# One program, two issue orders: instructions moved within the orders of all five engines of a hybrid decoder layer

## The chip, the cores and the metric

The kernel runs on one core of a Trainium2 chip. The metric is the device time of one execution in microseconds; the time of a kernel is the median of its runs. A profiled execution also leaves a trace, whose times are us from the start of its span. TensorE (PE) does the matrix products, with its weight loads (PEld) recorded beside them; VectorE (DVE), ScalarE (ACT) and GpSimd (POOL) work on tiles; SyncE (SP) issues the transfers (DMA).

## The reference

One layer of a decoder trunk, for 1024 tokens of 1024 channels, all float32. One input projection feeds three groups of heads, whose gated outputs go through one output projection, a residual and a LayerNorm:

```python
proj = jnp.einsum("bsd,de->bse", x, w_in[l])
q, k, v, g_a, x_b, g_b, c_cols, g_c = jnp.split(proj, split_idx, axis=-1)
y_a = _swa_sinks(q, k, v, attn_sinks[l])        # sliding-window attention: 8 q heads, 2 kv heads, d=64, window 128
y_b = _rg_lru(x_b, conv_w[l], ...)              # causal conv of 4, gates, linear recurrence h = a*h + u; 256 wide
y_c, v_own = _rwkv7(c_cols, rwkv_mu[l], ...)    # RWKV-7: token shift, decay, delta-rule matrix state; 4 heads of 64
y = jnp.concatenate([y_a * silu(g_a), y_b * silu(g_b), y_c * silu(g_c)], axis=-1)
out = jnp.einsum("bse,ed->bsd", y, w_out[l])
x = _layer_norm(ALPHA * x + out, ln_g[l], ln_b[l])
```

## The kernel before

**Arithmetic.** Each large product is computed in three parts: an operand is rounded to a shorter type (`xh`, `wcah`, `w_q`, on ScalarE or VectorE), the residue is taken on VectorE (`xl`, `wcal`, the lower half of `w_q`), and TensorE adds high by high, high by low and low by high into one PSUM tile (`mm3`, line 301). A product of one weight tile has 128 rows of contraction and 512 columns, half of the tokens.

**Stages.** The tokens are done in two halves (0 and 1) of 512. First come the projections of the RWKV group of half 0, straight from the weights in `in_w_c`, in eight steps k over the channels (tile `c`, lines 345 to 372). Then, for each half, a stream of dense projections runs (`pj_q`, `pj_ga`, `pj_xb` and so on), and between its products stand those of the attention (`sp`, `tp`, `pv`), the recurrence of group B (a scan on VectorE) and the RWKV group. The RWKV group computes in chunks of 64 tokens: scores within a chunk (`sc`, from `AR` and `BK`), an inverse of a triangular matrix (`rwkv_inverse`, `rwkv_merge`, which end in the tile `Tt`), and a chain over the eight chunks (`rwkv_chain`) that carries the state `S`: `S` times a tile goes through `UV` (copied by ScalarE or VectorE), a product `ch`, its copy `u`, another product `ch`, and so on to the next state. The projected weights that both halves need are split once and kept in DRAM (`kept_q`, `kept_ga`). Last comes the output projection `o` of both halves with residual and LayerNorm on VectorE.

**Start.** The input transfers are issued by SyncE in an order of its own. TensorE begins with four products of the tile `blocks` with itself, 256 columns, whose result nobody reads (`WARM = 4`, line 341); they are TensorE's numbers 0 to 3. `con` holds the constants, the identity for the transposes among them; `par` the per-channel parameters, from which VectorE computes columns `dv` and `sc`.

**Order.** What sets the order of the work is written out by hand twice. `MERGED` (line 58) gives the order in which the generators of the stages are asked for their next piece, and with it the order in which instructions are created, the tiles and the buffers. Then, for each of the five engines, `ISSUED` (line 67) says in which order its instructions are issued. `Listed` (line 223) stands before each engine and records its instructions as they are created; the numbers in `ISSUED` are positions in that record, and "4-6" stands for 4, 5, 6. At the end of the program the lists are turned into dependencies that cost no wait:

```python
for a, b in zip(seq, seq[1:]):
    tc.add_manual_dep(b, a.name, NOSYNC, reason="order of the engine")
```

Each engine works strictly down its list; where the next instruction isn't ready, all that stand behind it wait. Since every instruction goes through the one call in `Listed`, nearly all rows of the profile name line 231: what an instruction is, its tiles say.

Of the kernel before, what the change touches and what calls it, by code (L numbers as in the profile page):

```python
# [172 lines left out]
),  # L173
"gpsimd": (
    "0 2 1 3-4 14-15 5-13 17 16 27-28 18-24 26 25 29-37 41-48 39 38 40 49-52"
),
"sync": (
# [1159 lines left out]
```

## Time and profile before

| | |
|---|---|
| median of 3 runs | 482.28 us (481.49, 482.28, 482.39) |
| profiled execution, own time | 482.19 us |
| its span in the trace | 480.4 us |
| TensorE busy | 466.0 us, 97% of the span |
| VectorE busy | 364.7 us, 76% |
| ScalarE busy | 242.4 us, 50% |
| GpSimd busy | 36.4 us, 8% |
| DMA | 71.45 MB, mean 149 GB/s |

The profiled execution is one of many; its own time is that of the device, its span the part that the trace covers. Busy time of an engine is the time in which at least one of its instructions ran. Rows of the trace give the start of an instruction in us from the span's start and how long it was busy; TensorE's products overlap, so that the distance of two starts, not the busy time, tells how fast it goes.

### The profile page before, as it was taken

Reading aid. Unit: us, or ns where it says so; the run is one execution under the profiler, and the core shown is the slowest. Engines: PE = TensorE matmul, PEld = TensorE weight load, DVE = VectorE, ACT = ScalarE, POOL = GpSimd, SP = SyncE. Lnnn points to the kernel's source line nnn. Section 1 sums busy time; section 2 is a strip of 40 time slices with the busy share of each in tenths; the row PEclk is TensorE's granted clock in tenths of the full one; section 3 lists DMA queues with packets and bytes.
Section 4 is the critical chain, followed back from the end, with each engine's and each line's share of the span. In section 5 each row is a group of like instructions: output and inputs, shape, how many; then the busy total and the mean of one; then the engine's idle time right before and its main releaser. Section 6 shows DMA issues by size and latency. Waiting matters only on the chain.

```text
span 480.4 us, 8435 instructions
## 1 busy us (share of the span) xinstructions
PE 466.0 (97%) x3088; PEld 360.8 (75%) x3088; DVE 364.7 (76%) x880; ACT 242.4 (50%) x544; POOL 36.4 (8%) x57
## 2 busy tenths in 40 slices
PE   8999999999999999999999998999999999999993
PEld 6777777777777776678778786787678778888893
DVE  5946798999998689737979669994868548636886
ACT  3427589434566798537694255329666546021000
POOL 0100000000000000000000000000002500054101
PEclk9999999999999999999999999999999999999997
DMA  8950537657766524233343484459420080120652
GB/s 275 386 200 0 196 136 264 199 130 262 268 238 130 189 91 132 89 114 128 99 167 88 141 233 153 132 119 220 134 67 24 16 283 32 64 69 0 219 176 87
DMA packets 50585, 71.45 MB, mean 149 GB/s; under 512 B 26344, under 2 KB 27624, under 8 KB 50544
## 3 DMA queue, kind: packets, MB, share of 16 engines
q1 hardware_dynamic: 50544, 70.91, 46.3%
q8 instruction: 24, 0.39, 0.4%
q14 instruction: 17, 0.14, 0.1%
HBM read 48.34 MB, written 22.56 MB: 148 GB/s over the span
## 4 chain that ended last, share of the span: by engine, by line
PE 74%; DVE 9%; ACT 7%; DMA 6%; issue 2%; SPq 1%; POOLq 0%; DVEq 0%; ACTq 0%
PE o L231 19%; PE pj_q L231 8%; PE pj_ga L231 6%; PE c L231 6%; PE pj_xb L231 3%; PE pj_gb L231 3%; PE pj_gc L231 3%; PE sp L231 3%; PE pv L231 3%; PE pj_v L231 2%; PE pj_r L231 2%; PE ch L231 2%; PE pj_av L231 2%; PE tp L231 2%; PE pj_k L231 2%
## 5 line engine op out<-in xcount | busy, mean ns | idle before, releaser
L231 PE MATMUL pj_ga<-xh,w_ga 128*128 128x512 f32 x128 | 44.0, 404 | 0.9 <-DMA w_ga<-kept_ga 0.9
L231 PE MATMUL pj_q<-xh,w_q 128*128 128x512 f32 x128 | 44.1, 403 | 0.5 <-DMA w_q<-kept_q 0.2
L231 ACT ACTIVATE s<-sp,mn 128x129 f32<-128x129 f32 x64 | 23.0, 366 | 22.0 <-DVE mn L231 21.7
L231 PE MATMUL o<-woh,yl 128*128 128x512 f32 (+1 forms) x90 | 32.5, 370 | 0.0
L231 PE MATMUL o<-woh,yh 128*128 128x512 f32 (+1 forms) x90 | 32.5, 375 | 0.0
L231 PE MATMUL o<-wol,yh 128*128 128x512 f32 (+1 forms) x90 | 32.3, 368 | 0.0
L231 PE MATMUL o<-wo,yh 128*128 128x512 f32 (+1 forms) x108 | 32.0, 374 | 0.0
L231 PEld LDWEIGHTS pj_ga<-xh,w_ga 128*128 128x128 f32 x128 | 23.6, 188 | 7.6 <-DVE it L231 1.2
L231 POOL TENSOR_TENSOR yl<-y,yh 128x512 fp32r<-128x512 f32 x16 | 20.3, 1291 | 118.0 <-PE pj_gc L231 105.5
L231 PEld LDWEIGHTS pj_q<-xh,w_q 128*128 128x128 f32 x128 | 23.8, 188 | 7.0 <-DMA w_q<-kept_q 0.7
L231 DVE SCALAR_TENSOR_TENSOR xres<-xres,o 128x512 f32<-128x512 f32 (+1 forms) x18 | 11.1, 624 | 20.3 <-PE o L231 16.2
L231 PE MATMUL pj_ga<-xl,w_ga 128*128 128x512 f32 x64 | 25.9, 405 | 0.0
L231 PE MATMUL pj_q<-xl,w_q 128*128 128x512 f32 x64 | 25.7, 401 | 0.0
L231 ACT ACTIVATE s<-s,mn 128x128 f32<-128x128 f32 x64 | 22.3, 398 | 4.3 <-DVE mn L231 4.1
L231 DVE SCALAR_TENSOR_TENSOR xres<-xres,mv,ln 128x512 f32<-128x512 f32 x32 | 22.6, 741 | 1.0 <-POOL mv L231 0.9
L231 PE MATMUL pj_gc<-xh,w_gc 128*128 128x512 f32 x64 | 23.1, 414 | 0.2 <-DVE q L231 0.2
L231 ACT CAST yh<-y 128x512 fp32r<-128x512 f32 x16 | 9.7, 618 | 26.6 <-PE o L231 22.1
L231 PEld LDWEIGHTS o<-wo,yh 128*128 128x128 f32 x108 | 19.4, 188 | 4.2 <-DVE wo L231 0.3
L231 PE MATMUL pj_gb<-xh,w_gb 128*128 128x512 f32 x64 | 21.8, 404 | 0.0
L231 PE MATMUL pj_xb<-xh,w_xb 128*128 128x512 f32 x64 | 21.8, 399 | 0.0
L231 DVE TENSOR_TENSOR PT<-tp,con 128x512 f32<-128x512 f32 x28 | 19.1, 684 | 3.4 <-PE tp L231 3.2
L231 PE MATMUL o<-wo,yl 128*128 128x512 f32 (+1 forms) x54 | 19.8, 369 | 0.0
(310 smaller groups left out, 1247.1 us busy)
## 6 DMA issues: line engine op xcount, KB each, us to landing
xr<-in_xT SPq DMA_DIRECT2D x16, 256.0 KB, 4.5
kept_ga<-w_ga SPq DMA_DIRECT2D x8, 512.0 KB, 3.2
kept_q<-w_q SPq DMA_DIRECT2D x8, 512.0 KB, 3.5
wor<-in_w_o SPq DMA_DIRECT2D x16, 256.0 KB, 2.8
w_q<-kept_q SPq DMA_DIRECT2D x8, 512.0 KB, 3.9
w_ga<-kept_ga SPq DMA_DIRECT2D x8, 512.0 KB, 4.4
xres<-in_x SPq DMA_DIRECT2D x8, 512.0 KB, 3.6
out<-xres SPq DMA_DIRECT2D x16, 256.0 KB, 2.2
```

The lines of the kernel that those rows point to most:

```text
L231: self.ins.append(getattr(self.engine, op)(*args, **kw).ins)
```

## The change

Only the five lists in `ISSUED` are replaced. The same instructions are created in the same order (2460 on TensorE, 880 on VectorE, 468 on ScalarE, 53 on GpSimd, 226 on SyncE), with the same tiles, buffers and data dependencies; only the order in which each engine takes them is another. Counted against the longest common order of the old and the new list, 499 instructions of TensorE stand elsewhere (in 410 runs of one or more), 293 of VectorE (283 runs), 150 of ScalarE (150), 7 of GpSimd (6) and 65 of SyncE (63). Most moves are short: TensorE's number 7 goes from place 4 (counted from 0) to place 0, the warm-up products 0 to 3 from places 0 to 3 to places 3, 4, 8 and 10; VectorE's 57 from place 32 to 4, its 298 from 216 to 209, its 684 from 687 to 686; ScalarE's 177 from 180 to 176, so that it stands ahead of 115; SyncE's 11 (the transfer of `con`) from 2 to 32. The diff, cut to the lines in which these stand:

```diff
@@ -66,121 +66,138 @@
...
 ISSUED = {
 "tensor": (
-    "0-3 7 10-11 8 4-6 19-20 22-23 13 24-25 21 26 39-43 9 14-15 33-35 27 44-45 53-54 28-29 47 12 30-32 50-51 48 "
...
-    "1033 1013-1016 908-911 1017-1020 1036-1039 1034-1035 1044-1046 1053-1056 1049-1052 1084-1102 1047-1048 "
...
-    "1593-1623 1836-1839 1641 1835 1840-1841 1846 1642-1644 1628-1631 1847-1850 1662-1669 1851-1854 1546 "
...
+    "7 4 13 0-1 10-11 8 2 9 3 22-23 14 5-6 15 27 19-20 24-25 21 26 33-34 39 28 35 42 40 44 16 29 47 53 41 12 "
...
+    "1011-1012 1023 1041-1042 1024 903 990-997 1025 1043 1028 1044-1046 1029-1030 1047 1033 1013-1016 908-911 "
...
+    "1823-1824 1833-1834 1624-1625 1648-1651 1626-1627 1593-1623 1836-1841 1835 1846-1847 1641-1644 1628-1631 "
...
 ),
 "vector": (
-    "55-56 78 80 77 54 79 0-1 3 2 5 4 6-8 44 10 43 9 49 53 45 42 46 51 11 52 48 47 50 12 57 103 58 73 16 59 17 "
...
-    "125 132 128 131 129 252 126 156 209 264 141 143 234 142 235 144 257 146 236 147 251 149 148 439 210 157 211 "
-    "150 212 237 290 238 372 158 239-240 159 164 160 165-168 161-163 151 441 467 152 298 153 303 154 306 155 170 "
...
-    "392 360 339-340 337 370 341 343-344 338 413 345 342 347-349 346 351 417 361 418 350 390-391 295-296 362 "
...
-    "631 637 636 660 685 661 677 683 686 721-722 688 662-663 684 664 676 665-666 691-693 689 697-698 694 699 747 "
...
+    "0 56 1-2 57 3 78 52 43 77 5 79 58 46 6 45 4 8 7 10 51 103 53 42 49 9 55 54 11-12 50 59-60 16-17 61 13 62 80 "
...
+    "109 120 122 121 110 118 203 224 123 229 135 133 145 136 134 126-127 130 124 132 137 125 138 488 222 241 207 "
...
+    "157 150 237 290 238-239 211 572 439 212 158 372 240 159 441 164 160-161 467 165 298 166 162 303 167-168 163 "
...
+    "390-391 350 418 361 295-296 362 299-300 363 301-302 417 424 382 393 326 394-395 327 329-330 396 331 425 401 "
...
+    "683 661 721-722 688 662 684 663 665 664 691 676 692-693 689 697 694 698-699 747 700-703 717-719 678 704 720 "
...
 ),
 "scalar": (
-    "1 0 2-4 26 5 17 6-7 27 55-56 8-16 18-19 21 24-25 22 31 23 30 32 28 20 29 34-35 57 59-60 58 33 62 36 38-40 42 "
...
-    "107 112 175-176 115 185 116 118 177 179 178 194-195 181 140 196-197 141 221 145 222 219 180 206 225 165 164 "
-    "226 168 182 228 171 198-199 170 202 227 183 201 203 200 205 204 229 231 188 233 232 187 207 189 208 217 "
-    "209-210 237 213 234 212 235 214 247 252 248-249 224 223 230 218 254 236 238-240 253 241 264 243-244 266 242 "
...
+    "1 0 2-4 26 5-6 17 7 27 8 55 9 56 10-16 18-19 21 31 24-25 22 32 23 20 57 30 28 34-35 59 29 33 60 58 62 36 "
...
+    "175-177 115 185 179 118 116 221 178 180 194 141 195 140 197 196 222 145 181 219 206 164-165 225-226 168 182 "
+    "228 171 198-199 202-203 170 227 201 183 207 200 229 205 204 231 208 188 187 233 232 189 217 209-210 234 212 "
+    "235 214 213 247 237 252 248-249 224 223 230 218 254 238 236 239-240 253 241 243-244 264 266 242 245 250-251 "
...
 ),
 "gpsimd": (
-    "0 2 1 3-4 14-15 5-13 17 16 27-28 18-24 26 25 29-37 41-48 39 38 40 49-52"
+    "0 2 1 3-11 13 12 16-17 14-15 18-20 28 21-27 29-37 41-48 39 38 40 49-52"
 ),
 "sync": (
-    "0 2 11 1 3-6 10 28 7-9 13 12 14-16 29-31 17-22 33 32 23-26 44-45 34 46 48 27 47 50 52 51 53-54 49 35-36 "
...
+    "0 2 1 28 10 3-7 29 8-9 13 12 14-16 30 17-20 31-32 21-23 33 24-25 44 11 26-27 45 47 34 46 48 51 35 50 49 36 "
...
 ),
 }
```

## Rows read from the trace of the kernel before

**Rows 1.** The page's first part (busy us of an engine, its share of the span, its instructions) and the first line of its fourth (the chain of work that ended last, in shares of the span).

```profile
PE 466.0 (97%) x3088; PEld 360.8 (75%) x3088; DVE 364.7 (76%) x880; ACT 242.4 (50%) x544; POOL 36.4 (8%) x57
...
PE 74%; DVE 9%; ACT 7%; DMA 6%; issue 2%; SPq 1%; POOLq 0%; DVEq 0%; ACTq 0%
```

**Rows 2.** Busy time by stage (the windows view). Columns: the stretch in us from the span's start, its length, busy us (and instructions) of TensorE, its weight loads, VectorE, ScalarE, GpSimd, the granted TensorE clock, the DMA engines' share, GB/s.

```profile
17.00:45.00 28.00, 27.82 (x119) 21.97 (x120) 18.36 (x59) 11.46 (x21) 0.00 (x0) 1.00 0.48 184
45.00:160.00 115.00, 114.22 (x674) 87.09 (x673) 104.84 (x264) 72.38 (x164) 2.84 (x11) 1.00 0.63 199
160.00:206.00 46.00, 44.57 (x521) 31.24 (x522) 35.62 (x91) 34.66 (x87) 1.04 (x2) 1.00 0.34 109
...
290.00:345.00 55.00, 52.73 (x444) 40.27 (x442) 46.11 (x129) 28.52 (x72) 0.00 (x0) 1.00 0.58 155
...
403.00:472.70 69.70, 69.69 (x348) 58.42 (x346) 48.21 (x88) 7.59 (x13) 16.32 (x15) 1.00 0.27 92
```

**Rows 3.** TensorE's first instructions (the timeline of TensorE, 0 to 9.3 us): start, busy us, output tile from input tiles, shape, instructions that the row joins, and in brackets the idle time before and what ended it.

```profile
1.48 3.78 PE L231 MATMUL c<-blocks 128*128 128x256 f32 x8 [1.48 <-POOL blocks L231]
5.00 1.22 PE L231 MATMUL c<-xh,wcah 128*128 128x512 f32 x2
...
6.87 0.63 PE L231 MATMUL c<-xh,wcah 128*128 128x512 f32 x1
7.30 0.44 PE L231 MATMUL c<-xl,wcah 128*128 128x512 f32 x1
7.58 0.39 PE L231 MATMUL c<-xh,wcal 128*128 128x512 f32 x1
7.81 0.40 PE L231 MATMUL c<-xh,wcbh 128*128 128x512 f32 x1
```

**Rows 4.** The granted clock where TensorE starts and behind its last work (the windows view; the sixth column of figures after the length is the clock, as in rows 2).

```profile
5.00:7.39 2.40, 2.40 (x7) 1.93 (x7) 1.39 (x4) 0.76 (x2) 0.00 (x0) 1.00 0.92 272
...
475.00:480.40 5.40, 0.00 (x0) 0.00 (x0) 1.83 (x3) 0.00 (x0) 0.82 (x1) 0.50 0.26 97
```

**Rows 5.** Waits and transfers of the start: TensorE's weight load near 9.20 and its products at 16.33 and 17.18 (the timeline of 0 to 20 us); VectorE's first reading of `par` (the timeline of VectorE); the transfer of `con` in the chain that ended last (start, length); TensorE's transposes of v (the timeline of TensorE).

```profile
9.20 0.19 PEld L231 LDWEIGHTS c<-xh,wcah 128*128 128x128 f32 x1 [0.50 <-ACT wcah L231]
...
16.33 0.40 PE L231 MATMUL c<-xh,wcbh 128*128 128x512 f32 x1
...
17.18 0.50 PE L231 MATMUL c<-xh,wcal 128*128 128x512 f32 x1 [0.45 <-DVE wcal L231]
...
9.79 0.16 DVE L231 TENSOR_SCALAR dv<-par 128x2 f32<-128x2 f32 x1
...
1.65 4.01 DMA con<-in_con
...
58.09 0.60 PE L231 MATMUL vtp<-con,vt 128*128 128x128 f32 x4
```

**Rows 6.** Four waits of TensorE and the instruction that each waits for (timelines around 87, 108, 202 and 340 us, columns as in rows 3; in each the product before, the product that waited, and the releaser on VectorE or ScalarE).

```profile
86.49 0.74 DVE L231 SCALAR_TENSOR_TENSOR AR<-xs_k,par,W 128x512 f32<-128x512 f32 x1
...
86.73 0.39 PE L231 MATMUL pj_q<-xh,w_q 128*128 128x512 f32 x1
...
87.38 0.83 PE L231 MATMUL sc<-AR,BK 64*128 64x128 f32 x10 [0.26 <-DVE AR L231]
...
107.35 0.69 DVE L231 TENSOR_TENSOR w_q<-wr_q,w_q 128x512 fp32r<-128x512 f32 x1
107.50 0.40 PE L231 MATMUL pj_q<-xh,w_q 128*128 128x512 f32 x1
...
108.09 0.73 PE L231 MATMUL pj_q<-xh,w_q 128*128 128x512 f32 x2 [0.20 <-DVE w_q L231]
...
202.02 0.62 PE L231 MATMUL pj_k<-xh,w_k 128*128 128x512 f32 x2
202.87 0.34 PE L231 MATMUL ch<-UV,X 128*64 128x64 f32 x4 [0.23 <-ACT UV L231]
...
202.51 0.30 ACT L231 COPY UV<-S 64x128 f32<-64x128 f32 x1 [1.61 <-DVE S L231]
...
338.89 0.63 PE L231 MATMUL pj_ga<-xh,w_ga 128*128 128x512 f32 x2
340.26 0.35 PE L231 MATMUL ch<-u,Tt 64*64 64x64 f32 x5 [0.74 <-issue]
...
339.47 0.69 DVE L231 COPY Tt<-tp 32x512 f32<-32x512 f32 x1
```

**Rows 7.** ScalarE in the first recurrent chain: the copy `UV`, an exponential and the product `ch` that waits (timeline of 183.6 to 186.8 us); one tanh of 512 columns (timeline of ScalarE, 166.5 to 170); and all copies of this kind together (the view by lines: count, then busy us and mean ns, then idle time before them and what ended it).

```profile
184.05 0.30 ACT L231 COPY UV<-S 64x128 f32<-64x128 f32 x1 [0.39 <-DVE S L231]
184.25 0.36 ACT L231 ACTIVATE s<-sp,mn 128x129 f32<-128x129 f32 x1
...
184.40 0.70 PE L231 MATMUL ch<-UV,X 128*64 128x64 f32 x8
...
168.67 0.69 ACT L231 ACTIVATE tr<-lg,dv 64x512 f32<-64x512 f32 x1
...
L231 ACT COPY UV<-S 64x128 f32<-64x128 f32 x15 | 4.5, 297 | 6.1 <-DVE S L231 6.1
```

**Rows 8.** The end (timeline of 471.9 to 480.4 us): VectorE's residual that waits for TensorE's last product, and the last two scalings.

```profile
472.73 0.42 DVE L231 SCALAR_TENSOR_TENSOR xres<-xres,o 128x256 f32<-128x256 f32 x1 [0.47 <-PE o L231]
...
475.85 1.41 DVE L231 SCALAR_TENSOR_TENSOR xres<-xres,mv,ln 128x512 f32<-128x512 f32 x2 [0.44 <-POOL mv L231]
```

203 rows, old and new, of the table ISSUED are left out of this document.

## The prediction, as it was put on record before the change was run

> **What bounds the kernel now.** I read the page first, then the time by stage, then the start, then the places where TensorE waits. The page says what kind of kernel it is: TensorE is busy for 97% of the span and carries 74% of the chain that ended last; VectorE has 76%, ScalarE 50% [rows 1]. A change of orders takes no work away, so TensorE's own work stays, and only four things can move the end: its clock at the start, its waits, the work it has at the two ends, and new waits. The windows by stage say where there are waits at all: 28.00 us with 27.82 busy in the first projections, 114.22 of 115.00 in the second stage, 44.57 of 46.00 and 52.73 of 55.00 in the two with the recurrent chains and the inverses, and 69.69 of 69.70 in the output projection [rows 2]. The first of these is also the price of one product of 512 columns on a full clock: 27.82 / 119 = 0.234 us from start to start. Where a start comes later than that, TensorE waited; the start-to-start time less 0.234 is what I call the loss of a wait. Over the whole trace behind 45 us I found 26 losses over 0.15 us, 9.1 us together; the ones that carry the sum are in [rows 6, 7].
>
> The profiled execution took 482.19 us with a span of 480.4, so 1.8 us lie outside the span; the median of the runs is 482.28, and I make the sum against 482.19. About 0.2%, 1.0 us, is what a measurement of this kernel tells from no change.
>
> **Part 1, TensorE's start: +2.5 us (bounds +0.8 to +3.7).** Before, the four warm-up products (numbers 0 to 3) run from 1.48 on, when nothing else can; the first real product starts at 5.00, behind its cast [rows 3]. Starts of 512-column products lie 0.43 us apart until 7.30 and 0.23 from 7.58 on (6.87, 7.30; 7.58, 7.81) [rows 3]. [...] The level rose 7.4 − 1.48 = 5.9 us after TensorE's first work.
>
> After, the stream begins with 7, a real product which needs the same cast, so TensorE's first work begins at 5.00; the warm-ups stand as 0–1 behind 7, 4, 13, as 2 behind 8 and as 3 behind 9. Two costs follow. The warm-ups are now in line with real work: 3.78 / 4 = 0.94 us each at the lower level [rows 3], half of it at the full one, four of them 1.9 us. And the level: if it rises 5.9 us after the first work again, it rises at 10.9, 3.5 us later than before; in that time TensorE does half the work, so 1.75 us are lost. If it rises at 7.4 whatever was done, this is 0. On the other side stalls of the start go, because TensorE is now behind its data: the product at 17.18 started 0.85 after the one at 16.33, a loss of 0.62 (VectorE's `wcal`), one near 9.20 lost 0.2 to 0.5 (ScalarE's `wcah`) [rows 5]; with two smaller ones 1.1 us. So 1.9 + 1.75 − 1.1 = 2.5; without the clock's part 0.8; with no stall relieved 3.7. Behind 17 us TensorE has no gap before 45 [rows 2], so what is lost here is lost at the end.
>
> [...]
>
> The other moves of the start cost nothing, I think. SyncE issued the transfer of `con` as its third, at 1.65 [rows 5]; number 11 goes far back in its list, others come forward. `con` is first needed by the transposes into `vtp` at 58.09 [rows 5], tens of us later, so the move is covered; uncovered it would be one transfer, 4 us. VectorE's number 57, which computes from `par`, now comes fifth (before 33rd); it waits for `par` (first used at 9.79 [rows 5]), and the residues `wcal` queue behind it; TensorE, on the half clock with warm-ups among its products, covers that until about 10.
>
> **Part 2, waits of TensorE that get a margin: −5.7 us (bounds −2.9 to −5.7).** For each of the 26 losses I looked up which instruction of another engine it waited for, and where the two stand in the new lists. For 17 the releaser moves up or TensorE's instruction moves down by more than the loss. Four examples [rows 6]: at 87.38 `sc` starts 0.65 after 86.73 and waits for VectorE's `AR` (number 126, done 87.23), a loss of 0.42; behind the new lists it has some 12 us. At 108.09 a product waits for VectorE's residue `w_q` (298, done 108.04): 0.59 after 107.50, loss 0.36; 298 now comes about 3.5 us of VectorE work earlier. At 202.87 `ch` waits for ScalarE's `UV` (223, done 202.81): two products from 202.02 fill 0.47, so the loss is 0.85 − 0.47 = 0.38; 0.94 us of other products now stand ahead of it. At 340.26 `ch` waits for VectorE's copy `Tt` (684, done 340.16; the row names no releaser, but that end lies 0.10 before it): two products from 338.89, loss 1.37 − 0.47 = 0.90; 684 now comes one instruction of VectorE earlier, ahead of the scan that ran for 1.28 before it. By stages: 45 to 160, five waits, 1.68; 160 to 206, six, 2.20; 206 to 290, two, 0.35; 290 to 345, four, 1.49: together 5.7. The other nine (3.4 us) have the same releaser in the same place and stay. The end that I hold possible on the other side is half, 2.9, if half of what is relieved turns up as the next wait: VectorE is busy for 104.84 of 115.00 in the second stage [rows 2], and what it does earlier pushes something else later.
>
> **Part 3, new waits: +1.5 us (bounds 0 to 4.8).** In 160 to 206 TensorE goes round a chain with ScalarE: `UV` copied out, two products, `u` copied out. At 184.05 `UV` is copied, at 184.40 `ch` starts [rows 7]. In the new list of ScalarE other work comes ahead of such copies: a tanh (177, one of 0.69 like that at 168.67) ahead of the copy 115, an exponential (203, 0.36 like that at 184.25) ahead of 170, the copy of 184.05 [rows 7]. By the times of before, seven copies between 162 and 192 would come 0.26 to 0.70 late, 3.3 us together. But the 15 `UV` copies together waited 6.1 us for VectorE's `S` [rows 7], 0.4 each; work put ahead of a copy falls first into that wait. And TensorE's stream puts other products in between. I take 1.5, a bit under half of 3.3: nothing if all falls into the waits, 7 × 0.69 = 4.8 if none does.
>
> **The end: 0.** The output projection has no gap (69.69 of 69.70 [rows 2]), and behind its last product come VectorE's residual at 472.73 [rows 8], the statistics, two scalings from 475.85 and the store; the lists keep that order.
>
> Sum: 482.2 + 2.5 − 5.7 + 1.5 = **480.5 us**, a span of 478.7.
>
> **Rivals.** First, slower: ScalarE's work ahead of the chain's copies. If none of it falls into waits, part 3 is 4.8: 482.2 + 2.5 − 5.7 + 4.8 = 483.8. It makes the kernel slower once the new waits pass 3.2 + 1.0 = 4.2 us. For it: seven copies that move the wrong way. Against it: the 0.4 us of waiting before each. Chance 0.2. Second, no change: waits relieved come back as the next wait, because VectorE has little room: half of part 2, 482.2 + 2.5 − 2.9 + 0.5 = 482.3 (new waits are then a part of what came back, and 0.5 is what is left of them). For it: 104.84 of 115.00 [rows 2]. Against: the moved work has several us of margin in some places. Chance 0.2. Third, faster still: the clock rises at 7.4 as before and the start is nearly free: 482.2 + 0.8 − 5.7 + 1.5 = 478.8. For it: only that a single rise can't show what it hangs on; against: the row of the end, where the clock is at 0.50 without work [rows 4]. Chance 0.15. My forecast has 0.45.
>
> **How the numbers follow.** Forecast and third rival lie below 481.3: faster 0.6; the second rival is the same, 0.2; the first slower, 0.2. The range goes from 477.3 (third rival with no new waits) to 483.8 (first rival). The forecast's own range is 478.7 to 481.7, the clock's part of 1.75 to one side and 1.2 to the other.
>
> **What would show it.** In the profile after: products of 512 columns 0.43 us apart from 5.00 until about 11, no wait for `wcal` near 17, and the first projections ending some 2.5 us later than before. Then TensorE without waits at `sc` near 87, at the `w_q` product near 108, at `ch` near 203 and 340, so that the stage of the second inverse loses 1.5 us of its idle time. `UV` and `u` copies later behind their releasers in the first chain, at a cost of one to two us. The output projection 70 us and the tail 7.7, as before. It is wrong if the full clock comes at 7.4 though TensorE began at 5; if waits come up at places that had none, above all for VectorE; or if the first chain takes longer by more than 3 us.

## The result and the profile after

The changed kernel took 485.16 us (median of 5 runs, 484.91 to 486.76), before 482.39 (5 runs, 481.49 to 483.33) on the same chip: a ratio of 1.0064, 95% interval 1.0042 to 1.0085. It is 2.8 us slower, where 480.5 and a gain was forecast. Its profiled execution took 484.91 us with a span of 483.1, so 1.8 us lie outside the span as before. The mean granted clock was 0.995 or 0.996 in all five executions; in the trace of this one it is 1.00 in every stage up to 475 us and 0.74 behind TensorE's last work (475.5 to 483.1; compare [rows 4]), so the 2.8 us are not lost to a fall of the granted clock.

The first part of the page, after (compare [rows 1]):

```profile
PE 462.6 (96%) x3088; PEld 360.3 (75%) x3088; DVE 364.0 (75%) x880; ACT 239.6 (50%) x544; POOL 35.8 (7%) x57
```

Every engine has as many instructions as before; TensorE is busy for 3.4 us less in a span that is 2.7 longer. The time by stage (columns as in [rows 2]):

```profile
17.00:45.00 28.00, 28.00 (x122) 22.18 (x121) 16.10 (x58) 11.49 (x22) 0.00 (x0) 1.00 0.53 193
45.00:160.00 115.00, 113.09 (x660) 86.85 (x660) 106.45 (x269) 70.96 (x163) 4.01 (x13) 1.00 0.62 196
160.00:206.00 46.00, 44.34 (x538) 32.28 (x531) 34.31 (x87) 33.91 (x86) 0.00 (x0) 1.00 0.33 105
...
290.00:345.00 55.00, 51.77 (x427) 39.55 (x426) 45.18 (x128) 27.86 (x73) 0.00 (x0) 1.00 0.53 139
```

TensorE idles 1.91 us of the second stage instead of 0.78, and 3.23 between 290 and 345 instead of 2.27 [rows 2]. To see where the time goes I laid the two TensorE streams side by side by work done: each product counts with its usual distance to the next start, and at equal work I took the difference of the two times. This table is worked out so from the two traces; its figures are good to some 0.2 us:

| at (us of before) | 26 | 85 | 96 | 137 | 157 | 185 | 205 | 264 | 284 | 294 | 334 | 345 | 372 | 410 | end |
|---|---|---|---|---|---|---|---|---|---|---|---|---|---|---|---|
| after is behind by | 0.75 | 0.6 | −0.3 | 0.7 | 0.5 | 2.3 | 0.6 | 0.4 | 0.2 | 1.6 | 2.9 | 1.6 | 2.2 | 2.5 | 2.7 |

The start costs 0.75; between 26 and 284 gains and losses nearly cancel (0.6 are won); between 284 and the end 2.5 us are lost. One trace of each is little for the first of these: compared at 26 us in the same way, the traces of eight runs below whose lists begin as before's lie between 0.3 ahead of before and 0.7 behind it, and those of four runs that begin as after's lie 0.6 to 0.8 behind. The start of after is slower, by about 0.6. The tail from VectorE's last residual on is the same: 475.46 to 483.1, 7.6 us [rows 8].

**Most waits that were to go are gone.** TensorE after, at the four places of [rows 6], and at `w_ga`, for which it waited at 297.63 before:

```profile
85.77 0.88 PE L248 MATMUL sc<-AR,BK 64*128 64x128 f32 x5
...
107.54 0.86 PE L248 MATMUL pj_q<-xh,w_q 128*128 128x512 f32 x3
...
204.54 0.45 PE L248 MATMUL ch<-UV,X 128*64 128x64 f32 x8
...
342.06 0.45 PE L248 MATMUL ch<-u,Tt 64*64 64x64 f32 x8
...
298.46 0.39 PE L248 MATMUL pj_ga<-xh,w_ga 128*128 128x512 f32 x1
```

No bracket with idle time stands behind any of them; losses of 0.42, 0.36, 0.38, 0.90 and 1.14 have become 0.1 or nothing. Over all instructions that waited over 0.15 in either trace, the losses that shrank sum to −6.1 us. The 1.14 of w_ga is a part of that, and no relief: its transfer is issued at 293.89 after and at 293.50 before, and TensorE only comes to it later, behind new waits. Nor can the prediction have counted it, since its four waits between 290 and 345 sum to 1.49 with the 0.90 of 340.26 among them. So at most 5.0 of the 5.7 came out. **And others came.** The largest in the trace of after (timelines of TensorE around each place):

```profile
110.88 0.50 PE L248 MATMUL sp<-KH,q 128*128 128x128 f32 x2 [0.61 <-DVE q L248]
...
158.91 0.58 PE L248 MATMUL gp<-T,X 32*32 32x32 f32 x13 [0.80 <-DMA T<-dT]
...
287.88 0.55 PE L248 MATMUL bt<-con,BK 128*128 128x128 f32 x3 [0.68 <-ACT BKt L248]
...
292.24 0.33 PE L248 MATMUL vp<-con,xs_v 128*128 128x128 f32 x1 [0.47 <-ACT BKt L248]
...
301.12 0.36 PE L248 MATMUL sp<-KH,q 128*128 128x256 f32 x1 [1.00 <-DVE PT L248]
...
336.55 0.22 PE L248 MATMUL tp<-Tt,Gp 32*32 32x32 f32 x2 [1.47 <-DMA Tt<-dTt]
```

The losses that grew sum to 10.8 us by the same count, and only a part of them lies in the chain of 160 to 206, where the prediction looked for them. (Waits under 0.15 fall by 2.7 in sum, so that 45 to the end costs 2.0.) The one of 336.55 has its cause in SyncE's list. SyncE before, then after, around the second inverse (the list's numbers are 170, 169; 171; 184; 173, 172, 174 before, and 169; 173; 170; 183; 174, 171, 172 after):

```profile
326.74 0.85 SPq L231 DMA_DIRECT2D T<-dT  x2
327.63 0.49 SPq L231 DMA_DIRECT2D Tt<-dTt  x1
328.16 0.49 SPq L231 DMA_DIRECT2D w_ga<-kept_ga  x1
328.69 1.50 SPq L231 DMA_DIRECT2D Tt<-dTt  x3
```

```profile
328.26 0.32 SPq L248 DMA_DIRECT2D T<-dT  x1
328.64 0.48 SPq L248 DMA_DIRECT2D Tt<-dTt  x1
329.17 0.49 SPq L248 DMA_DIRECT2D T<-dT  x1
329.69 0.49 SPq L248 DMA_DIRECT2D w_ga<-kept_ga  x1
330.23 1.49 SPq L248 DMA_DIRECT2D Tt<-dTt  x3
```

TensorE's first product on Tt reads block 171. Before, it is the lone one at 327.63; after, it is the second of the three from 330.23, issued 3.1 us later: 1.5 because the whole group starts later, the rest by its place behind two other blocks of Tt and a load of w_ga.

### The profile page after: what moved, and what is told of

Same layout as the page of the kernel before. It is cut to its first block, busy times and chain, and to the rows that moved or that the text cites. A ratio compares the mean times of both kernels' runs of the same rounds, so it can differ in the third digit from the quotient of the medians.

```text
span 483.1 us, 8447 instructions
## 1 busy us (share of the span) xinstructions
PE 462.6 (96%) x3088; PEld 360.3 (75%) x3088; DVE 364.0 (75%) x880; ACT 239.6 (50%) x544; POOL 35.8 (7%) x57
## 4 chain that ended last, share of the span: by engine, by line
PE 76%; DVE 11%; DMA 5%; ACT 3%; issue 2%; SPq 1%; POOLq 0%; DVEq 0%; ACTq 0%
PE o L248 19%; PE c L248 8%; PE pj_ga L248 6%; PE pj_q L248 5%; PE pj_xb L248 4%; PE pj_gb L248 4%; PE pj_gc L248 3%; PE ch L248 3%; PE pj_k L248 3%; PE pj_ak L248 2%; PE pj_v L248 2%; PE pj_r L248 2%; PE pj_av L248 2%; PE sp L248 2%; PE tp L248 2%
## 5 line engine op out<-in xcount | busy, mean ns | idle before, releaser
L248 PE MATMUL pj_ga<-xh,w_ga 128*128 128x512 f32 x128 | 45.4, 408 | 0.2
L248 PE MATMUL o<-wo,yh 128*128 128x512 f32 (+1 forms) x108 | 33.9, 372 | 0.2 <-ACT wo L248 0.2
L248 ACT ACTIVATE s<-s,mn 128x128 f32<-128x128 f32 x64 | 23.3, 397 | 5.4 <-DVE mn L248 5.1
L248 DVE SCALAR_TENSOR_TENSOR xres<-xres,mv,ln 128x512 f32<-128x512 f32 x32 | 23.9, 776 | 1.7 <-POOL mv L248 1.5
L248 PE MATMUL pj_gb<-xh,w_gb 128*128 128x512 f32 x64 | 23.0, 408 | 0.0
L248 PE MATMUL sp<-KH,q 128*128 128x256 f32 (+1 forms) x64 | 17.6, 297 | 2.2 <-DVE PT L248 1.0
```

The source lines that it names most:

```text
L248: self.ins.append(getattr(self.engine, op)(*args, **kw).ins)
```

## The experiments

Theory A: each new wait has a cause of its own, an instruction or a transfer that now stands too far back; put it forward and the time comes back. Theory B (the second rival, grown): the stages are paced by series of work away from TensorE (VectorE's steps of the inverse and the transfers behind them, ScalarE's copies, reloaded weights); a relief ahead of such a place is handed back there, and what delays the place costs in full. Each run was timed beside before on one chip, not always the same; behind its time stands its ratio to before with the 95% interval. In the diffs, numbers are positions as in the lists. "Behind by" is the comparison at equal work, as in the table above. The mean granted clock of an execution tells whether the clock fell in the middle of it: it was 0.994 to 0.997 in all executions of before that these runs are compared with, and 0.985 to 0.992 in the executions whose traces show such a fall.

**The start.** Warm-ups back to the head of after's list:

```diff
 "tensor": (
-    7 4 13 0-1 10-11 8 2 9 3 22-23
+    0-3 7 4 13 10-11 8 9 22-23
...
```

> After, with TensorE's four warm-up products put back to the head of its list and nothing else. In the traces after is 0.75 us behind before at 25 us and stays so to 60. If the warm-up products in line cost that (0.21 to 0.43 us for each of eight records, less the waits for data that vanish behind them), this is 0.4 to 0.8 below after, 484.4 to 484.8, with waits for wcah and wcal back near 9 and 17. If the place of the warm-ups is nothing and the late 0.75 comes from the other moves of the start, it is as after, 485.2.

485.56 us, 1.0083 (1.0056 to 1.0110): no gain in the median. In its trace TensorE is 0.9 ahead of after at 16 us and still 0.8 at 157; so the warm-ups in line cost 0.8 there, as expected. Then it comes to the product on T, waits 0.66 and 0.19 us for it, and what follows is in the windows:

```profile
156.00:160.00 4.00, 3.15 (x84) 2.36 (x83) 2.75 (x6) 2.41 (x8) 0.00 (x0) 1.00 1.13 297
160.00:164.00 4.00, 4.00 (x76) 3.00 (x74) 0.70 (x1) 3.57 (x8) 0.00 (x0) 0.55 0.15 51
164.00:168.00 4.00, 4.00 (x28) 2.73 (x26) 1.81 (x4) 0.71 (x2) 0.00 (x0) 0.59 0.00 0
```

The granted clock is 0.55 and 0.59 on the mean of the two windows behind the waits, and 1.8 us are lost: more than the start had given. Another 0.8 goes at 399.47, where TensorE waits for ScalarE's `gsh`. The three executions of this kernel without such a fall (0.995 and 0.996) took 484.2 to 485.4.

The warm-ups spread in before:

```diff
 "tensor": (
-    0-3 7 10-11 8 4-6
+    7 0-1 10-11 2-3 8 4-6
...
```

> Before, with the four warm-up products put into the stream of real ones (order 7, 0, 1, 10, 11, 2, 3, 8), so that TensorE has no work before about 4.6 to 5.0 us, as in after. My prediction's first part (the level rises as long after the first work as before, 5.9 us): the full clock comes near 10.7, 1.9 + 1.75 - 1.1 = 2.5 us slower, 484.9. What the profile of after shows instead (0.43 us between starts until 7.4, 0.23 from 8.1): the full clock comes near 8, and the products in line cost 8 x 0.43 = 3.4 less what lay idle before (3.1 + 0.6 of waits for data): 0.3 to 0.8 us slower, 482.7 to 483.2.

483.71 us, 1.0032 (1.0019 to 1.0045), behind by 2.0 at 26 us and by 1.8 at the end. TensorE's first rows:

```profile
4.64 0.80 PE L231 MATMUL c<-xh,wcah 128*128 128x512 f32 x1 [4.64 <-DVE xl L231]
...
9.93 0.60 PE L231 MATMUL c<-xh,wcah 128*128 128x512 f32 x1
10.36 0.41 PE L231 MATMUL c<-xl,wcah 128*128 128x512 f32 x1
10.60 0.39 PE L231 MATMUL c<-xh,wcal 128*128 128x512 f32 x1
```

From 9.93 to 10.36 0.43, then 0.24: the full pace at about 10.4, 5.7 us after the first work. In after it came earlier:

```profile
4.59 1.65 PE L248 MATMUL c<-xh,wcah 128*128 128x512 f32 x3 [4.59 <-ACT wcah L248]
6.04 1.91 PE L248 MATMUL c<-blocks 128*128 128x256 f32 x4
7.38 0.90 PE L248 MATMUL c<-xh,wcah 128*128 128x512 f32 x1
8.12 0.63 PE L248 MATMUL c<-xl,wcah 128*128 128x512 f32 x2
8.59 0.59 PE L248 MATMUL c<-blocks 128*128 128x256 f32 x2
```

The records from 5.18 to 7.32 lie 0.43 apart, the two from 8.12 on 0.24: the full pace at about 8, 3.4 us after the first work. So the rise is neither at a fixed time (7.4 before, about 8 and 10.4 here) nor a fixed time after the first work (5.9, 3.4, 5.7). (It is read from the starts alone: the windows print a granted clock of 1.00 on both sides of it, from 0 to 9 us in before and from 0 to 20 in after.) The rise isn't even the same for the same start. These are the same two products in two runs below that begin with the lists of before, both with the first work near 1.48 (timelines of TensorE):

```profile
5.73 0.63 PE L231 MATMUL c<-xl,wcah 128*128 128x512 f32 x2
```

```profile
5.91 1.05 PE L231 MATMUL c<-xl,wcah 128*128 128x512 f32 x2
```

They start 0.24 us apart in the first and 0.43 in the second. In the nine traces with this start (before's among them) the full pace comes at 5.1 to 5.5 in four and at 7.0 to 7.5 in five; in the five with the start of after it comes at about 8. The early rise gains nothing that shows at 26 us: the four lie from 0.3 ahead of before to 0.4 behind it, the five from 0.3 ahead to 0.7 behind.

After's order in the stretch until 45 us alone, in before:

```diff
 all five lists
-before
+after's order for what before starts until 45 us, then before's
```

> Before, with the five lists of after for what before starts ahead of 45 us only. By the trace of after the start alone is 0.75 us slower: 482.9. With the full clock as late as in the run where only the four warm-ups were spread (10.3 us), 484.

484.41 us, 1.0049 (1.0036 to 1.0062). In its trace it is behind by 0.74 at 26 us, as after is; another 1.3 us come at the seam, where TensorE waits 1.15 us for VectorE's `xs_v` at 49.24, a wait that after doesn't have. Part of this run's loss is the seam's.

**The transfers of T and Tt.** In after, the order of before within their places:

```diff
 "sync": (
...
-    80 81 108 82 110 78 79 83
+    83 79 108 78 110 82 80 81
...
-    180 169 173 170 183 174 171 172
+    180 170 169 171 183 173 172 174
...
```

> After, with one change: in SyncE's list the six transfers that bring the first inverse's halves T and Tt back into the chip (78 to 83), and the six of the second inverse (169 to 174), stand in the places that they have, but in the order of before (the T halves and the Tt block that TensorE uses first come first). In the profile of after TensorE waits 0.86 + 0.16 us at 158.9 for T and 1.72 at 336.55 for Tt. Theory A (specific: a transfer put behind others that nobody waits for yet): both waits go, up to the next thing that is late (ScalarE's copy of Gp ends at 335.30, 0.5 us after TensorE was free), so 1.0 + 1.2 = 2.2 us less than after, about 482.9. Theory B (diffuse: VectorE is the limit, a wait that is taken away comes back at the next place): at most 0.5 less, about 484.7.

487.65 us, 1.0116 (1.0101 to 1.0131): slower than after. Near 337 the loss at Tt falls from 1.72 to 0.57 (1.2 us), 0.4 of it goes by 341, and at 346.27 TensorE loses 0.89 instead of 0.09 to ScalarE's copy `UV`: by 349 all of the 1.2 is handed back. At 158 the loss at T falls by 0.3, a later product then loses 1.0 to VectorE's PT, and the granted clock is 0.65 and 0.50 in the windows 160 to 164 and 164 to 168. That place alone sets this run 2.3 us behind after, nearly all that it is slower in its trace; the one execution of 0.996 took 486.38. Theory A's gain isn't there: the 1.2 won at Tt is handed back. Why the place at 158 got worse with its own order of before isn't shown.

The opposite, in before:

```diff
 "sync": (
...
-    180 183 170 169 171 184 173 172 174
+    180 183 169 173 170 184 174 171 172
...
```

(The first inverse's six likewise.)

> Before, with the opposite change: the twelve transfers of T and Tt take the order of after within their places. Theory A: T of the first inverse lands 1 to 1.5 us later and TensorE waits up to 1 us near 158, the first block of Tt of the second inverse is issued 1.5 to 2 us later and TensorE waits 1.3 to 1.7 more near 333.6; 484.0 to 485. Theory B: it is within 0.5 of before, 482 to 483.

485.13 us, 1.0073 (1.0049 to 1.0096). In its trace the first inverse's order changed nothing. The second's is this (timeline of TensorE, then windows):

```profile
332.05 0.63 PE L231 MATMUL pj_ga<-xh,w_ga 128*128 128x512 f32 x2
335.35 0.28 PE L231 MATMUL tp<-Tt,Gp 32*32 32x32 f32 x2 [2.66 <-DMA Tt<-dTt]
```

```profile
332.00:336.00 4.00, 1.34 (x6) 0.82 (x6) 3.43 (x6) 3.88 (x7) 0.00 (x0) 0.84 0.60 145
336.00:340.00 4.00, 4.00 (x56) 3.04 (x57) 0.84 (x3) 0.57 (x1) 0.00 (x0) 0.50 0.01 4
340.00:344.00 4.00, 4.00 (x42) 2.88 (x39) 3.82 (x6) 1.09 (x2) 0.00 (x0) 0.50 0.00 0
344.00:348.00 4.00, 4.00 (x40) 2.73 (x39) 1.42 (x4) 2.29 (x4) 0.00 (x0) 0.88 0.61 196
```

The wait costs 2.4 us more than the 0.4 of before, and from within it on the clock is at half for some 10 us (by the four windows), which costs 2.8 more. Executions of this kernel with a mean granted clock of 0.994 to 0.996 took 483.1 to 484.3 us, those of 0.985 and 0.986 487.3 to 488.6. The order of six transfers does it alone, by the wait and in a part of the executions by a fall of the clock too: here Theory A holds. What was a relief in the one direction is no mirror of the loss in the other.

**Stretches alone.** Before until 275 us, after behind it; the same with the six transfers of the second inverse in before's order; after until 275, before behind it; after only from 45 to 275; and after with before's order from 275 to 297:

```diff
 all five lists
-before
+before until 275 us, after behind it
...
 "sync": (
-    180 169 173 170 183 174 171 172
+    180 170 169 171 183 173 172 174
...
 all five lists
-before
+after until 275 us, before behind it
...
 all five lists
-before
+before, with after's order from 45 to 275 us
...
 all five lists
-after
+after, with before's order from 275 to 297 us
```

> All five lists of before for everything that before starts ahead of 275 us, and behind it all five lists of after. The traces put the loss of after there: 0.6 us behind at 274, 2.7 at the end. If the places behind 275 cost this by themselves (transposes bt and vp that wait for ScalarE's copies at 287.9 and 292.2, 1.5 us together; Tt of the second inverse behind other transfers at 336.6), this is 2.1 us slower than before, 484.3. If after's late part is slow only because of what came ahead of it, it is as before, 482.2.

486.55 us, 1.0108 (1.0082 to 1.0134). The waits of after at 288, 292 and 301 are there with about the same lengths, and the one for Tt with 2.07 idle, 2.3 lost. Four of its six executions had a mean clock of 0.984 to 0.993; the two of 0.996, the profiled one among them, took 485.6 and 485.9, some 4 us above before.

> Before until 275 us and after behind it, as in an earlier run (486.6), with one change: SyncE's six transfers of T and Tt of the second inverse in the order of before within their places. TensorE waited 2.32 us at 337.3 for Tt there. If the order of the transfers is what makes after's late part slow, 1.5 to 2.3 less, 484.3 to 485.1. If ScalarE's copies are late in any case (as in the first run, where the wait came back at 345), 486.

484.71 us, 1.0058 (1.0045 to 1.0072), 1.8 less than without; all its executions had 0.994 or 0.995, so only about 1 of the 1.8 stands against executions of the same clock. In the traces 1.7 are won at 335, and 1.15 handed back by 345, most of it at 343.77, where TensorE now waits 0.71 for ScalarE's `UV`, as it did at 346 in after with before's order of the transfers. That order is a cause of the late loss, not the only one.

> The complement: the lists of after until 275 us, of before behind it. By the same traces 0.6 us slower than before (the start's 0.75 and a zero sum of waits between 45 and 275), 482.8; if the stretch of the first inverse near 160 is the place that loses (in two of the last profiles the granted clock fell there to 0.50 behind TensorE's wait for T), 483.5 to 485 with a wide spread.

483.74 us, 1.0034 (1.0017 to 1.0051); its profiled execution took 482.67 and is behind by 0.5.

> Before, with the five lists of after for what before starts between 45 and 275 us only. The traces give after 0.1 to 0.2 us of gain there in sum (0.9 to 1.2 won near 90 and at 185 to 205, lost near 130, at 158 for T, at 180). If after's middle is neutral, 482.0; if the wait for T near 158 makes the granted clock fall in a part of the runs, a median of 483 with a spread of 2 us.

482.99 us, 1.0021 (1.0010 to 1.0032). By its trace it is ahead by 0.2 at 274: the middle's reliefs and new waits cancel in that execution; the median is 1.2 us above before, and executions with a clock of 0.991 and 0.992 took 483.3 to 484.0, those of 0.996 481.4 to 483.5.

> After, with the five orders of before for what after starts between 275 and 297 us. The two waits of TensorE for ScalarE's copies BKt there (0.84 and 0.63 us) should go, so 1.5 less than after, 483.7, if it is kept; 485 if it comes back further on (the next wait, for VectorE's PT at 301.1, is 1.16 long and takes up to that much).

484.99 us, 1.0068 (1.0047 to 1.0089): nothing gained. The two waits for `BKt` are gone, 1.45 us by 294; then TensorE waits 0.57 at 297.62, at the product on w_ga for which it waited in before, so that wait comes back as soon as the new ones ahead of it go, and 0.49 for w_q at 308.35. At 334 it is still 0.7 ahead of after. The rest goes behind its wait for Tt at 335.50, with the clock:

```profile
336.00:340.00 4.00, 4.00 (x76) 3.05 (x77) 2.78 (x5) 3.00 (x5) 0.00 (x0) 0.62 0.16 60
```

The four executions of 0.995 and 0.996 took 484.4 to 485.1, so nothing is gained without that fall either.

Start, middle and late part alone cost 2.4, 1.0 and 5.2 us by their ratios, 8.6 together; the whole change costs 2.8 to 3.1. Of the surplus 1.3 is the seam at 49 and about 1 the clock's in the late part (5.2 against some 4 in the executions of 0.996). For the rest, delays of one part fall into the waits of the next, as at w_ga; that this accounts for all of it isn't shown.

**Only the reliefs.** Before with five of the moves from which the prediction took its gain:

```diff
 "vector": (
...
-    129 252 126
+    126 129 252
...
-    151 441 467 152 298
+    298 151 441 467 152
...
-    417 361 418 350 390-391
+    390-391 417 361 418 350
...
-    663 684
+    684 663
...
 "scalar": (
-    233 232 187
+    187 233 232
```

> Before, with only the moves on VectorE and ScalarE from which my prediction took most of its gain: VectorE's 684 ahead of the scan 663, 390 and 391 ahead of 417, 298 ahead of 151, 126 ahead of 129; ScalarE's 187 ahead of 233. The waits of TensorE that they end were 0.90 (340.3), 0.43 (159.7), 0.36 (108.1), 0.42 (87.4) and 0.47 (191.1), 2.6 us. Theory A (what is relieved is kept): 479.6. Theory B (it comes back at the next wait, because the moved work now delays others on a busy engine): 481.5 to 482.5.

487.10 us, 1.0095 (1.0071 to 1.0118), 5 us above before. VectorE and TensorE near 160 (timelines of each):

```profile
155.19 0.69 DVE L231 TENSOR_TENSOR PT<-tp,con 128x512 f32<-128x512 f32 x1 [0.46 <-PE tp L231]
158.13 1.39 DVE L231 SCALAR_TENSOR_TENSOR q<-pj_q,q 64x512 fp32r<-64x512 f32 x2 [2.24 <-ACT q L231]
...
160.27 0.69 DVE L231 TENSOR_TENSOR PT<-tp,con 128x512 f32<-128x512 f32 x1
```

```profile
161.02 0.66 PE L231 MATMUL pv<-PT,vtok 128*64 128x128 f32 x8 [2.62 <-DVE PT L231]
```

390 and 391 were moved ahead of four instructions that were ready, and their own input, ScalarE's `q`, wasn't: it ended at 158.1. VectorE stood for 2.24 us with its whole list behind it, TensorE for 2.62, which sets it 2.3 us behind by 160, and the clock (0.50 from 164 to 168) adds 1.7; the one execution without that fall (0.995) took 483.90. In after the same move does little harm: ScalarE's list was moved too, its `q` ends at 157.20, and VectorE waits 0.27 for it. The other reliefs (87, 108, 191, 340) took effect in this trace and were handed back in whole or in part: a loss of 0.46 at 90.7 and of 0.71 at 110.5 for VectorE, 1.46 instead of 1.14 at 300.8 for w_ga, 0.8 instead of 0.15 for T at 335, 0.4 for `woh` at 400.7.

Before with one transfer put forward:

```diff
 "sync": (
...
-    160 182 163
+    160 163 182
...
```

> Before, with one move in SyncE's list: 163, the transfer of w_ga for which TensorE waits 1.14 us at 297.63, goes ahead of 182, the transfer of wor_0. In the trace of before 182 stood in the queue until 293.0 for VectorE, and 163 behind it, though its buffer was free at 291.9. Theory A (a wait that is taken away is a gain): 1.1 us faster, 481.0 against 482.1. Theory B (the stage is paced by VectorE's steps, which end when they end): the wait moves on to the next product that needs VectorE, at 300.1, where it grows from 0.56 to about 1.2; 0.3 to 0.6 faster, 481.6.

482.14 us, 0.9999 (0.9989 to 1.0009). The 1.14 are gone; eight products further on the wait for ScalarE's `s` has grown (timelines of TensorE, before and this run):

```profile
297.63 0.47 PE L231 MATMUL pj_ga<-xh,w_ga 128*128 128x512 f32 x1 [0.90 <-DMA w_ga<-kept_ga]
...
300.13 0.38 PE L231 MATMUL sp<-KH,q 128*128 128x256 f32 x1 [0.40 <-ACT s L231]
```

```profile
299.07 0.39 PE L231 MATMUL pj_ga<-xl,w_ga 128*128 128x512 f32 x1
300.55 0.38 PE L231 MATMUL sp<-KH,q 128*128 128x256 f32 x1 [1.08 <-ACT s L231]
```

A loss of 0.56 has become 1.24 there, and 0.4 more went near 400. Theory B, with a smaller gain than it allowed.

This, and the reliefs that had done no harm:

```diff
 "sync": (
-    160 182 163
+    160 163 182
 "vector": (
-    129 252 126
+    126 129 252
...
-    663 684
+    684 663
 "scalar": (
-    233 232 187
+    187 233 232
```

> Before, with the move of 163 and those reliefs of the earlier run that put nothing ahead of an instruction whose inputs are late: VectorE's 684 ahead of 663, 126 ahead of 129, ScalarE's 187 ahead of 233. Without the two that run showed to be harmful (390 and 391, which wait for ScalarE's q with all of VectorE's list behind them, and 298 ahead of the inverse). Theory A: 1.14 + 0.90 + 0.42 + 0.47 = 2.9 us faster, 479.2. Theory B: a third of that or less, 481.2 to 482.1; no fall of the granted clock near 160.

481.64 us, 0.9992 (0.9982 to 1.0002), not clear of no change. Ahead by 1.9 at 343, by 0.75 at the end: 0.4 is handed back to ScalarE's `s` at 345, 0.5 to ScalarE's cast `woh` at 396. And with these places moved too:

```diff
 "vector": (
-    560 568-570 613-614 571 615
+    613-615 560 568-571
 "sync": (
-    202 205 200-201 195-197
+    195-197 202 205 200-201
```

> The version of the four reliefs, with the two places opened at which its gain came back. In its trace TensorE waited 1.09 us at 298.8 for the exponential behind VectorE's 613 to 615, which stood behind four steps of the inverse although their input was there at 295.4: they go ahead of 560. And 0.36 us near 396 for ScalarE's cast of wor, whose transfer (195, issued at 387.8, landed at 395.4) ran beside the residual's and the two broadcast loads of the LayerNorm's factors, which nobody needs before 411: these four go behind 197. If the waits are taken away at the pacing places themselves, the gain stays: 1.09 + 0.36 to 0.9 more than the 0.5 of that run, 480.3 to 480.9. If the next pacing place (T of the second inverse near 330, ScalarE's s at 345) takes it back, 481.5.

481.62 us, 0.9990 (0.9979 to 1.0001): against before no difference that can be measured; by the ratios it is some 3.5 us faster than after. The wait at 298.8 is gone and TensorE is 2.55 ahead by 303; then:

```profile
304.67 0.63 PE L231 MATMUL pj_xb<-xh,w_xb 128*128 128x512 f32 x2
306.34 0.44 PE L231 MATMUL tp<-con,s 128*128 128x128 f32 x2 [1.05 <-ACT s L231]
```

1.2 are handed back within 10 us to the next exponential of the same attention head, 0.5 more behind 345; 1.2 are left of 2.55 in this execution.

**One engine's list alone.** After with SyncE's list of before, and before with TensorE's list of after:

```diff
 after's lists
-"sync": after
+"sync": before
...
 before's lists
-"tensor": before
+"tensor": after
```

> After, with SyncE's whole list of before (65 moves undone). If SyncE's order carries the loss of the late part (the order of Tt alone cost before 2.4 us of waiting at 333), the wait of 1.72 at 336.6 goes and most of it is kept: 483 to 484. If TensorE's waits come back at ScalarE's copies, as in the first run of this study (where 1.2 of 1.2 came back at 345): 485.

506.60 us, 1.051 (1.0486 to 1.0535): the largest waits behind the start are 4.4 us for w_gc, 3.1 for w_gb, 2.9 for w_ga.

> Before, with TensorE's list of after and all else as it was. By my prediction the moves on TensorE relieve only two of the named waits (202.9 and 87.4, 0.8 us), and its start costs 0.75 to 2: 482.5 to 484. If TensorE's new order was made for other orders on VectorE and ScalarE, TensorE's waits grow by several us and the clock falls in places: over 486.

508.10 us, 1.0541 (1.0515 to 1.0566): behind the start 3.8 us for VectorE's `M`, 2.4 for `AR`, 3.3 in six waits for ScalarE's `s`. Each list fits the four others: one that is out of step with them costs 24 to 26 us against before, where all five together cost 3.

## Why the prediction was wrong

In the prediction's own terms the sum came out as +0.75 for the start, −6.1 for the waits that shrank, +10.8 for those that grew, −2.7 for the small ones and 0 for the tail: 2.75 instead of −1.7. The step that failed is part 3, the new waits, put at 1.5 and at most 4.8; and with it the assumption of part 2 that at least half of a removed wait stays won.

**Part 1 (+2.5, bounds 0.8 to 3.7)** had the right mechanism and one term too large. The warm-ups in line and the vanished waits came out (no wait for `wcal` near 17, [rows 5] answered by a stage without idle time); the clock's 1.75 did not. It rested on a rise 5.9 us after the first work in after too, the author's estimate from the one rise in [rows 3], and no run shows this term. In after the pace of the starts rose 3.4 us after the first work, with a granted clock of 1.00 on both sides, and the start cost 0.75, near the third rival's 0.8. In before with the warm-ups spread the pace rose after 5.7, and there the start cost 2.0. The rise can't be read off one trace: with one and the same start it came after 3.7 to 4.0 us in four traces and after 5.6 to 6.0 in five. The 0.75 lies at the lower bound; the value taken was too high. (A smaller slip: a warm-up product is two records, and by their starts, 0.43 apart, 0.86 us at the lower level, not 0.94.)

**Part 2 (−5.7)** was right in most of what it counted and wrong in what it concluded. Of the 5.7 at most 5.0 went (−6.1 less the 1.14 at w_ga), but a wait that goes isn't a gain until the next instruction with an input from elsewhere has been looked at. The reliefs that were tried without the other moves came back in large part: of the 1.14 at w_ga 0.68 at the next exponential and 0.4 near 400, of 2.55 by 303 1.2 at 306. The lower bound of half was still too hopeful; the four runs with reliefs alone came out 5 us above before (some 4 of it from one harmful move), level with it, and 0.5 and 0.2 below it, neither of these clear of no change.

**Part 3 (+1.5, bounds 0 to 4.8)** is the step that failed: the losses that grew sum to 10.8 us. New waits were searched only on ScalarE and only between 160 and 206. There the chain did lose 1.8 us until 185 and got it back by 205: the first rival's mechanism, at no cost in the end. The others were outside: transfers of T and Tt, ScalarE's copies of `BKt` (at 287.88 TensorE's new order asks for one sooner, at 292.24 the copy itself begins 0.9 us later than before), VectorE's `q` and `PT`. Of SyncE's 65 moves the prediction priced the one of `con`; the one whose place costs 2.4 us of waiting in before, and 1.2 in after, is the block 171 of Tt, put behind three transfers that TensorE wasn't waiting for yet.

**The end (0)** was right for the output projection and the tail. But between 345 and 410, where the prediction had no term, 0.9 us went, 0.4 of it at 348.4, 0.2 at 351.5 and 0.3 near 395 (ScalarE's `wo`).

**The rivals.** The second named the mechanism, waits that come back at the next limit, and stopped it at half. Together with new waits that no relief explains, it is what happened. What would have told for the reliefs: after each relieved wait, the next releaser's end time in the trace, where that doesn't move with TensorE.

**Open.** How the 2.8 us divide over the moves isn't settled: the stretches alone sum to three times as much, and to about twice as much without the seam and the clock's part. Nor is it shown why after kept its clock at 158 (1.00 in its trace, a mean of 0.995 or 0.996 in all five executions), while four of five executions with before's order of T (0.989 to 0.993), and three of six with the warm-ups first (0.985 to 0.992), had a lower one; the traces of these two lost it there.

## What to carry to other kernels

A wait in a trace was worth no more here than the slack of the next instruction that waits for somebody else (of the 1.14 at w_ga 0.68 came back at ScalarE's `s`); walk on from it and add up until the pace is set by an engine or a transfer that TensorE's earlier arrival doesn't move. When an order is changed, price every transfer by who needs it first, and never put an instruction ahead of ready ones on a strict list unless its own inputs are early too (390 and 391 held VectorE up for 2.24 us). Issue orders of several engines are one object (one list out of step cost 24 to 26 us): judge all lists together.

## What the runs showed of the hardware

In some of these runs the granted clock fell in the middle of the kernel too. In before with after's order of the transfers it was 0.84, 0.50, 0.50 and 0.88 in four windows of 4 us, the first of which holds TensorE's wait of 2.66 us. In after with the warm-ups first it was 0.55 and 0.59 behind waits of 0.66 and 0.19 us at the 64 products of 32 columns (3.15 of 4.00 us busy). The same place in after, with one wait of 0.80 and 2.20 of 3.00 us busy, kept 1.00:

```profile
157.00:160.00 3.00, 2.20 (x68) 1.63 (x69) 2.44 (x5) 1.57 (x7) 0.00 (x0) 1.00 1.13 294
160.00:163.00 3.00, 2.92 (x79) 2.15 (x74) 0.85 (x2) 2.92 (x7) 0.00 (x0) 1.00 0.38 109
```

So in the trace of before with after's order of the transfers a late transfer cost 2.4 us of waiting and 2.8 more behind it. Its executions with a mean clock of 0.985 and 0.986 took 487.3 to 488.6 us, those of 0.994 to 0.996 only 483.1 to 484.3. A fall stood behind the wait of 2.66 us and behind those of 0.66 and 0.19; behind the 0.80 of after it didn't come, as the last two rows show, nor behind its 1.47 at 336.55 (1.00 in the windows 332 to 336 and 336 to 340). So the length of a wait alone doesn't tell whether the clock falls; what does isn't shown.
